# The block norms of a decoder: sums by a wide product with ones, roots on wide tiles, instead of narrow products and a chain on a few columns

## The chip, the core and the metric

The kernel runs on one core of a Trainium2 chip. The core has five engines that work through their own queues, each in order: TensorE (PE in the profile; its weight loads are shown as PEld), VectorE (DVE), ScalarE (ACT), GpSimd (POOL) and SyncE (SP), which here issues transfers. They meet through semaphores. Operands lie in SBUF, products land in the eight banks of PSUM. The metric is the device time of one launch in microseconds (us); lower is better.

## The reference, cut to what matters

Two layers over 528 tokens (16 meta tokens and 512 others) of width 1024: a gated linear attention layer, then a sliding-window attention layer. Each layer has a half-step SwiGLU block, a mixer, and another half-step SwiGLU block, and each of these six blocks has a norm ahead of it and one behind it.

```python
def rmsnorm(x, g):
    xf = x.astype(jnp.float32)
    y = xf * lax.rsqrt(jnp.mean(xf * xf, axis=-1, keepdims=True) + EPS)
    return (y * g.astype(jnp.float32)).astype(x.dtype)
...
    for layer in range(DEPTH):
        g = norm_gains[layer]
        h = h + 0.5 * rmsnorm(swiglu(rmsnorm(h, g[0]), w_ffn_in[layer, 0], w_ffn_out[layer, 0]), g[1])
        hn = rmsnorm(h, g[2])
        ...
        h = h + rmsnorm(mix, g[3])
        h = h + 0.5 * rmsnorm(swiglu(rmsnorm(h, g[4]), w_ffn_in[layer, 1], w_ffn_out[layer, 1]), g[5])
        if layer == N_A_LAYERS - 1:
            k_sh, v_sh = shared_kv(h, kv_norm, w_kv, cos, sin)
```

What matters here is `rmsnorm` over the 1024 features of each token. The linear attention has a further norm per head over 256 features (`g_head`), which the change leaves as it is.

## The kernel before

Activations are kept transposed: the residual `H` and a block's output `Y` are tiles of 128 partitions by 8 slices by 528 tokens, so that a token is a column and its 1024 features lie on 128 partitions and 8 slices. A norm therefore has to add over partitions, and its factor has to be the same on all partitions of a column.

Every block product is made of three TensorE instructions of the rounded type fp32r: weights and activations are split into a high part (a copy on ScalarE) and a low part (the difference, on VectorE), and high x high, low x high and high x low are added in PSUM (`mm3s`). The large SwiGLU products use seven half-size products instead of eight (`Strassen`); their operands are called a, c, d and e.

Tokens are worked on in two groups: 0 to 271 and 272 to 527 in the first layer (272 and 256 tokens), 16 to 271 and 272 to 527 in the second (256 each). The last products of a block run for group 0 first and for group 1 then, and the first products of the next block (`x_first`) in the same order, so that the norm of one group runs while TensorE multiplies for the other.

A pre-norm scales nothing ahead of the products: `Operand.build` writes H times gain, split in two, and the root factor of each token is put into a tile R (`Operand.factors`), with which the results are multiplied when they are taken out of PSUM (the evacuations). A post-norm (`Residual.run`) multiplies Y by its factor, adds that to H, and builds the next block's operand slice by slice, eight slices k for a group.

The sums of squares are gathered by `square_into`: ScalarE squares each slice, GpSimd adds slices 0 to 6 into one tile `acc_..._0`, and the last slice has its own tile `acc_..._7`. Two tiles with 128 partitions of partial sums are left. From there `rstd` goes in three trips:

- narrow products `st`: for every chunk of 68 or 128 tokens, each tile of sums is loaded as weights and one column of ones is moved, which gives the sums with tokens on partitions (a tile of 68 x 4 or 128 x 2);
- a root of ten small operations on that tile (a guess from the bits and two steps of refinement), on VectorE for post-norms and for the opening, on GpSimd for the other pre-norms, with ScalarE taking the sum out of PSUM; then `dg`, which spreads the factors onto a diagonal;
- the product `r`: ones as weights, `dg` moved as n fp32 columns, which puts each token's factor on all partitions. It stays in PSUM; a pre-norm copies it to R.

The order of the work is the program's own. `Flow` keeps a clock that every product pushes on; jobs (generators) `yield` a delay and come up again when the clock has passed it, between the products of the block that is being issued. `DCHAIN` and `CHAIN` are the delays between `st` and `r` (for the root on VectorE and on GpSimd), `FACT` is the one ahead of a pre-norm's sums. A job's instructions stand in each engine's queue where it came up.

Names in the profile: `acc_post`, `st_post_l0m`, `r_post_l0m` belong to a post-norm (l0m: the one whose result is the next operand l0m), `acc_l0m`, `st_l0m`, `r_l0m` to a pre-norm; `t_...` is a post-norm's scaled output, `x_l0m` an operand's slices, `x` the first products of a block, `y` its last ones, `gu` the gate and up parts. In the profile l0f stands for both SwiGLU operands of the first layer, l1f for those of the second. ScalarE needs a table load (ACT_TABLE_LOAD) when the next function isn't in the loaded table; such loads are put into the program when it is built.

Of the kernel before, what the change touches and what calls it, by code (L numbers as in the profile page):

```python
# [40 lines left out]
DCHAIN = 3.0  # L41
FACT = 1.5
# [83 lines left out]
def trunk_kernel(ctx: ExitStack, tc, a, out):  # L126
# [19 lines left out]
    def ps(name):  # L146
        return pp.tile([P, 512], F32, tag="ps", name=name)
# [203 lines left out]
    def rstd(sq, n, dim, half, name, eng=pool):  # L351
# [11 lines left out]
        if eng is dve:  # L363
            dve.tensor_scalar(aa, st[:c, :nch], 1.0 / dim, 1e-6, op0=ALU.mult, op1=ALU.add)
        else:
            act.activation(aa, st[:c, :nch], AF.Identity, scale=1.0 / dim, bias=eps[:c])
        eng.tensor_scalar(yy.bitcast(I32), aa.bitcast(I32), -0.5, RSQRT_MAGIC, op0=ALU.mult, op1=ALU.add)

        eng.tensor_tensor(zz, yy, yy, op=ALU.mult)
        eng.tensor_tensor(zz, zz, aa, op=ALU.mult)  # L370
        eng.tensor_scalar(ww, zz, 0.375, -1.25, op0=ALU.mult, op1=ALU.add)
        eng.tensor_tensor(ww, ww, zz, op=ALU.mult)
        if eng is dve:
            dve.scalar_tensor_tensor(yy, ww, 1.875, yy, op0=ALU.add, op1=ALU.mult)
            dve.tensor_tensor(zz, yy, yy, op=ALU.mult)
            dve.scalar_tensor_tensor(zz, zz, -0.5, aa, op0=ALU.mult, op1=ALU.mult)
            dve.scalar_tensor_tensor(yy, zz, 1.5, yy, op0=ALU.add, op1=ALU.mult)
        else:
            pool.tensor_scalar(ww, ww, 1.875, None, op0=ALU.add)
            pool.tensor_tensor(yy, yy, ww, op=ALU.mult)  # L380
            pool.tensor_tensor(zz, yy, yy, op=ALU.mult)
            pool.tensor_tensor(zz, zz, aa, op=ALU.mult)
            pool.tensor_scalar(zz, zz, -0.5, 1.5, op0=ALU.mult, op1=ALU.add)
            pool.tensor_tensor(yy, yy, zz, op=ALU.mult)
        dg = sm.tile([P, 272], F32, tag="dg", name=f"dg_{name}", bufs=2)
        eng.tensor_tensor(
            dg[:c, :n].rearrange("p (j c) -> p j c", c=c),
            (hident if half else ident)[:c, :c].unsqueeze(1).to_broadcast([c, nch, c]),
# [3 lines left out]
        yield DCHAIN if eng is dve else CHAIN  # L392
        r = ps(f"r_{name}")
        mm(r[:, :n], ones[:c, :], dg[:c, :n])
        return r

# [16 lines left out]
    class Operand:  # L413
# [25 lines left out]
        def factors(self, gi, eng=pool):  # L439
# [11 lines left out]
    class Residual:  # L451
        def __init__(self, name, layer, i, half, nxt=None):
            self.name, self.half, self.nxt = name, half, nxt
            self.gain = lambda m: gain(layer, i, m)
# [942 lines left out]
```

## Time and profile before

| | |
|---|---|
| median of 3 runs | 1922.35 us (1922.07 to 1923.58) |
| profiled execution | 1923.81 us |
| its span on the core | 1922.0 us |
| mean granted TensorE clock | 0.993 of full |
| TensorE busy | 1886.6 us |
| VectorE, ScalarE, GpSimd busy | 1340.6, 993.8, 342.2 us |
| table loads on ScalarE | 7, of 1283 ns each |

The span is what the profiler saw on the core; the profiled execution's own time has 1.8 us around it. Busy times are sums over instructions of one engine; products are pipelined, so that what a product costs its successors is read from the distance of starts rather than from its own length. A wait is put down to what came last.

### The profile page before, as it was taken

What the parts mean: (1) busy time and instruction counts of PE and PEld (TensorE: products, weight loads), DVE (VectorE), ACT (ScalarE), POOL (GpSimd) and SP (SyncE); (2) the same over time, 40 slices, a digit from 0 to 9 for tenths busy, and PEclk for the clock granted to TensorE, in tenths of its full rate; (3) what the DMA queues carried; (4) which work ended last, traced back from release to release, by engine and by line L of the source; (5) the groups of instructions that cost most, each with busy time, mean ns of one, the idle gap of its engine ahead of it and who ended that gap; (6) DMA issues with size and microseconds to landing.
All of it is one profiled execution on the core that took longest, in us unless ns stands there. A gap on an engine that the chain in (4) does not pass through costs nothing.

```text
span 1922.0 us, 37874 instructions
## 1 busy us (share of the span) xinstructions
PE 1886.6 (98%) x14522; PEld 1800.2 (94%) x14522; DVE 1340.6 (70%) x2724; ACT 993.8 (52%) x2268; POOL 342.2 (18%) x561
## 2 busy tenths in 40 slices
PE   8999999999999999999999999999998999999997
PEld 8999999999999999999999898989976898989897
DVE  7884848676364787575877775858678778758484
ACT  5662626553245556353674563636645665636363
POOL 2101010311111400101034011010352141010102
PEclk9999999999999999999999999999998999999998
DMA  5555556222113245555542356565321215565651
GB/s 180 149 154 141 154 143 171 96 78 77 35 56 111 64 113 149 149 149 149 159 161 56 98 146 157 143 159 165 111 67 34 71 47 128 148 150 159 152 143 45
DMA packets 133253, 231.29 MB, mean 120 GB/s; under 512 B 14928, under 2 KB 27728, under 8 KB 133072
## 3 DMA queue, kind: packets, MB, share of 16 engines
q1 hardware_dynamic: 112048, 190.99, 30.8%
q0 software_dynamic: 20736, 37.76, 12.4%
q8 instruction: 113, 1.85, 0.4%
q14 instruction: 68, 0.56, 0.1%
q10 hardware_dynamic: 288, 0.13, 0.0%
HBM read 226.72 MB, written 2.10 MB: 119 GB/s over the span
## 4 chain that ended last, share of the span: by engine, by line
PE 89%; DVE 5%; ACT 2%; POOL 1%; issue 1%; DMA 0%; SPq 0%; DVEq 0%; POOLq 0%; ACTq 0%
PE y L164 31%; PE a L164 21%; PE x L164 16%; PE c L164 9%; PE d L164 5%; PE o L164 1%; DVE w L229 1%; PE e L164 1%; PE po L164 1%; ACT w L228 1%; PE sc L164 1%; PE ps L164 0%; DVE x_l0f L429 0%; PE st_go L164 0%; DVE H L468 0%
## 5 line engine op out<-in xcount | busy, mean ns | idle before, releaser
L254 POOL DMA_DIRECT2D raw<-in_w_in x144 | 126.1, 934 | 968.8 <-DMA raw<-in_w_in 530.0
L249 DVE TENSOR_TENSOR w_s<-raw,w_s 128x512 fp32r<-128x512 f32 x288 | 195.0, 689 | 109.3 <-ACT w_s L248 107.7
L164 PE MATMUL y<-hidl0f,w 128*128 128x272 f32 (+1 forms) x2112 | 260.9, 285 | 0.0
L164 PEld LDWEIGHTS y<-hidl0f,w 128*128 128x128 f32 x2112 | 258.8, 188 | 0.2
L229 DVE TENSOR_TENSOR w<-raw,w 128x512 fp32r<-128x512 f32 x378 | 243.4, 672 | 21.0 <-ACT w L228 19.1
L164 PE MATMUL y<-hidl1f,w 128*128 128x512 f32 (+1 forms) x1344 | 249.5, 346 | 0.0
L164 PEld LDWEIGHTS y<-hidl1f,w 128*128 128x128 f32 x1344 | 212.2, 188 | 33.4 <-ACT hidl1f L410 0.3
L248 ACT ACTIVATE w_s<-raw 128x512 fp32r<-128x512 f32 x288 | 177.7, 625 | 109.0 <-DVE raw L264 69.3
L228 ACT ACTIVATE w<-raw 128x512 fp32r<-128x512 f32 x378 | 208.1, 587 | 35.0 <-PE y L164 29.3
L249 DVE TENSOR_TENSOR w<-raw,w 128x512 fp32r<-128x512 f32 x216 | 145.4, 688 | 37.6 <-ACT w L248 35.9
L164 PE MATMUL x<-x_l0m,w 128*128 128x272 f32 (+1 forms) x1200 | 158.3, 288 | 0.0
L248 ACT ACTIVATE w<-raw 128x512 fp32r<-128x512 f32 x216 | 130.4, 621 | 48.0 <-PE y L164 44.6
L164 PEld LDWEIGHTS x<-x_l0m,w 128*128 128x128 f32 x1200 | 149.4, 188 | 1.2
L590 DVE TENSOR_TENSOR Y<-y,Y 128x256 f32<-128x256 f32 (+2 forms) x176 | 82.2, 474 | 92.3 <-PE y L164 91.9
L164 PE MATMUL a<-zl0f_t,w_s 128*128 128x264 f32 x864 | 117.0, 285 | 0.0
L164 PE MATMUL a<-zl1f_t,w_s 128*128 128x256 f32 x864 | 114.3, 281 | 0.8 <-ACT c L783 0.8
L164 PEld LDWEIGHTS a<-zl0f_t,w_s 128*128 128x128 f32 x864 | 110.1, 188 | 0.0
L164 PEld LDWEIGHTS a<-zl1f_t,w_s 128*128 128x128 f32 x864 | 107.0, 188 | 2.0 <-ACT c L783 2.0
L164 PE MATMUL x<-x_l0f,w 128*128 128x256 f32 (+1 forms) x768 | 101.1, 292 | 7.4 <-ACT w L228 6.1
L406 POOL TENSOR_TENSOR acc_post<-acc_post,sq_post 128x256 f32<-128x256 f32 (+1 forms) x72 | 58.0, 805 | 280.5 <-ACT sq_post L405 280.0
L164 PEld LDWEIGHTS x<-x_l0f,w 128*128 128x128 f32 x768 | 97.8, 194 | 8.6 <-ACT w L228 6.1
L164 PE MATMUL x<-x_l1f,w 128*128 128x256 f32 (+1 forms) x576 | 92.9, 320 | 0.0
(487 smaller groups left out, 3404.4 us busy)
## 6 DMA issues: line engine op xcount, KB each, us to landing
raw<-in_w_in SPq DMA_DIRECT2D x424, 256.0 KB, 3.6
raw<-in_w_in POOLq DMA_DIRECT2D x144, 256.0 KB, 4.9
raw<-in_w_out SPq DMA_DIRECT2D x96, 256.0 KB, 3.4
raw<-in_gla_in SPq DMA_DIRECT2D x50, 256.0 KB, 3.1
raw<-in_w_last SPq DMA_DIRECT2D x48, 256.0 KB, 3.3
raw<-in_w_out SPq DMA_DIRECT2D x64, 128.0 KB, 2.9
raw<-in_gla_out SPq DMA_DIRECT2D x16, 256.0 KB, 2.7
raw<-in_w_q SPq DMA_DIRECT2D x16, 256.0 KB, 4.0
```

What stands on the lines that cost most here:

```text
L164: inst = pe.matmul(o, lhs, rhs, start=start, stop=stop, skip_group_check=onto)
L228: act.activation(w[:, 0, :m], raw[:, :m], AF.Copy)
L229: dve.tensor_tensor(w[:, 1, :m], raw[:, :m], w[:, 0, :m].bitcast(F32), op=ALU.subtract)
L248: act.activation(w[:, 0, :512], src, AF.Copy)
L249: dve.tensor_tensor(w[:, 1, :512], src, w[:, 0, :512].bitcast(F32), op=ALU.subtract)
L254: pool.dma_start(dst, src, accum_op=ALU.add)
L406: pool.tensor_tensor(sums[0][:, :n], sums[0][:, :n], t[:, :n], op=ALU.add)
L590: dve.tensor_tensor(y, p[:, :n], y, op=ALU.add)
```

## The change

The norms over 1024 features (24 counted by group: 12 behind blocks, 12 ahead of them) get a new function `roots`. The two tiles of sums are now the moved operand: ones (128 x 128) as weights, n fp32 columns of each tile, both added in one bank. That gives each token's sum on all partitions at once, so that `dg` and `r` fall away. The root is taken on the wide tile: ScalarE's function Abs_reciprocal_sqrt gives a first value, its square on ScalarE and three VectorE operations refine it by one step, and the factor one half of a half-step block is a constant of the refinement. The result lies in SBUF: for a pre-norm in R itself, for a post-norm in the tile that held the last sum. In `Residual.run` the scaled output t takes turns in the two halves of the bank that held the sums.

The delays change: the roots come up `SUMMED` = 2.5 after the sums (it was 3.0 or 5 up to r), and a pre-norm's sums come up `FACT` = 5.0 after its last slice (it was 1.5). The per-head norms of the linear attention (`rstd`, names `go`) stay on GpSimd.

```diff
--- before.py
+++ after.py
@@ -38,8 +38,8 @@
 CHAINS = 2
 
 CHAIN = 5
-DCHAIN = 3.0
-FACT = 1.5
+SUMMED = 2.5
+FACT = 5.0
 START = 1.0
 SECOND = 6.0
 STATE_KEYS = 1.5
@@ -348,7 +348,7 @@
         mm3s([(o, w)], j, x, g, start, stop)
 
 
-    def rstd(sq, n, dim, half, name, eng=pool):
+    def rstd(sq, n, dim, name):
         c = 128 if n % 128 == 0 else n // 4
         nch = n // c
         st = ps(f"st_{name}")
@@ -360,39 +360,44 @@
         zv = sm.tile([P, 4], F32, tag="zv", name=f"zv_{name}")
         wv = sm.tile([P, 4], F32, tag="wv", name=f"wv_{name}")
         aa, yy, zz, ww = av[:c, :nch], yv[:c, :nch], zv[:c, :nch], wv[:c, :nch]
-        if eng is dve:
-            dve.tensor_scalar(aa, st[:c, :nch], 1.0 / dim, 1e-6, op0=ALU.mult, op1=ALU.add)
-        else:
-            act.activation(aa, st[:c, :nch], AF.Identity, scale=1.0 / dim, bias=eps[:c])
-        eng.tensor_scalar(yy.bitcast(I32), aa.bitcast(I32), -0.5, RSQRT_MAGIC, op0=ALU.mult, op1=ALU.add)
-
-        eng.tensor_tensor(zz, yy, yy, op=ALU.mult)
-        eng.tensor_tensor(zz, zz, aa, op=ALU.mult)
-        eng.tensor_scalar(ww, zz, 0.375, -1.25, op0=ALU.mult, op1=ALU.add)
-        eng.tensor_tensor(ww, ww, zz, op=ALU.mult)
-        if eng is dve:
-            dve.scalar_tensor_tensor(yy, ww, 1.875, yy, op0=ALU.add, op1=ALU.mult)
-            dve.tensor_tensor(zz, yy, yy, op=ALU.mult)
-            dve.scalar_tensor_tensor(zz, zz, -0.5, aa, op0=ALU.mult, op1=ALU.mult)
-            dve.scalar_tensor_tensor(yy, zz, 1.5, yy, op0=ALU.add, op1=ALU.mult)
-        else:
-            pool.tensor_scalar(ww, ww, 1.875, None, op0=ALU.add)
-            pool.tensor_tensor(yy, yy, ww, op=ALU.mult)
-            pool.tensor_tensor(zz, yy, yy, op=ALU.mult)
-            pool.tensor_tensor(zz, zz, aa, op=ALU.mult)
-            pool.tensor_scalar(zz, zz, -0.5, 1.5, op0=ALU.mult, op1=ALU.add)
-            pool.tensor_tensor(yy, yy, zz, op=ALU.mult)
+        act.activation(aa, st[:c, :nch], AF.Identity, scale=1.0 / dim, bias=eps[:c])
+        pool.tensor_scalar(yy.bitcast(I32), aa.bitcast(I32), -0.5, RSQRT_MAGIC, op0=ALU.mult, op1=ALU.add)
+
+        pool.tensor_tensor(zz, yy, yy, op=ALU.mult)
+        pool.tensor_tensor(zz, zz, aa, op=ALU.mult)
+        pool.tensor_scalar(ww, zz, 0.375, -1.25, op0=ALU.mult, op1=ALU.add)
+        pool.tensor_tensor(ww, ww, zz, op=ALU.mult)
+        pool.tensor_scalar(ww, ww, 1.875, None, op0=ALU.add)
+        pool.tensor_tensor(yy, yy, ww, op=ALU.mult)
+        pool.tensor_tensor(zz, yy, yy, op=ALU.mult)
+        pool.tensor_tensor(zz, zz, aa, op=ALU.mult)
+        pool.tensor_scalar(zz, zz, -0.5, 1.5, op0=ALU.mult, op1=ALU.add)
+        pool.tensor_tensor(yy, yy, zz, op=ALU.mult)
         dg = sm.tile([P, 272], F32, tag="dg", name=f"dg_{name}", bufs=2)
-        eng.tensor_tensor(
+        pool.tensor_tensor(
             dg[:c, :n].rearrange("p (j c) -> p j c", c=c),
-            (hident if half else ident)[:c, :c].unsqueeze(1).to_broadcast([c, nch, c]),
+            hident[:c, :c].unsqueeze(1).to_broadcast([c, nch, c]),
             yy.unsqueeze(2).to_broadcast([c, nch, c]),
             op=ALU.mult,
         )
-        yield DCHAIN if eng is dve else CHAIN
+        yield CHAIN
         r = ps(f"r_{name}")
         mm(r[:, :n], ones[:c, :], dg[:c, :n])
         return r
+
+
+    def roots(sums, n, c, name, dst=None):
+        s = ps(f"st_{name}")
+        for i, t in enumerate(sums):
+            mm(s[:, :n], ones, t[:, :n], i == 0, i == len(sums) - 1)
+        yield SUMMED
+        q, y = sums[0][:, :n], sums[1][:, :n] if dst is None else dst
+        act.activation(y, s[:, :n], AF.Abs_reciprocal_sqrt, scale=1.0 / D, bias=eps)
+        act.activation(q, y, AF.Square, scale=D ** -0.5)
+        dve.scalar_tensor_tensor(q, s[:, :n], D * 1e-6, q, op0=ALU.add, op1=ALU.mult)
+        dve.tensor_scalar(q, q, -0.5 * c, 1.5 * c, op0=ALU.mult, op1=ALU.add)
+        dve.tensor_tensor(y, q, y, op=ALU.mult)
+        return y, s
 
 
     def square_into(sums, src, i, count, name):
@@ -436,13 +441,12 @@
             o, n = self.groups[gi]
             square_into(self.accs[gi], H[:, k, o : o + n], k, KD, f"{self.name}_{o}_{k}")
 
-        def factors(self, gi, eng=pool):
+        def factors(self, gi):
             if self.rt is None:
                 self.rt = sm.tile([P, TOK], F32, tag="R", name=f"R_{self.name}", bufs=2)
             o, n = self.groups[gi]
             yield FACT
-            r = yield from rstd(self.accs[gi], n, D, False, f"{self.name}_{o}", eng)
-            act.activation(self.rt[:, o : o + n], r[:, :n], AF.Copy)
+            yield from roots(self.accs[gi], n, 1.0, f"{self.name}_{o}", self.rt[:, o : o + n])
 
         def need(self, gi, k):
             flow.until(lambda: (gi, k) in self.ready)
@@ -450,21 +454,22 @@
 
     class Residual:
         def __init__(self, name, layer, i, half, nxt=None):
-            self.name, self.half, self.nxt = name, half, nxt
+            self.name, self.c, self.nxt = name, 0.5 if half else 1.0, nxt
             self.gain = lambda m: gain(layer, i, m)
 
         def run(self, gi, g, sums):
             o, n = g
             nxt = self.nxt
             yield 1.8
-            r = yield from rstd(sums, n, D, self.half, f"post_{self.name}{gi}", dve)
+            r, s = yield from roots(sums, n, self.c, f"post_{self.name}{gi}")
             if nxt is None:
                 yield from self.store(gi, g, r)
                 return
             for k in range(KD):
                 h, y = H[:, k, o : o + n], Y[:, k, o : o + n]
-                t = r[:, 256 : 256 + n] if n <= 256 else ps(f"t_{self.name}{gi}{k}")[:, :n]
-                dve.tensor_tensor(t, y, r[:, :n], op=ALU.mult)
+                c = k % 2 * 256
+                t = s[:, c : c + n] if n <= 256 else ps(f"t_{self.name}{gi}{k}")[:, :n]
+                dve.tensor_tensor(t, y, r, op=ALU.mult)
                 dve.tensor_tensor(h, t, h, op=ALU.add)
                 nxt.build(gi, k)
                 nxt.sumsq(gi, k)
@@ -473,7 +478,7 @@
 
         def store(self, gi, g, r):
             o, n = g
-            rb = r[:, :n].unsqueeze(1).to_broadcast([P, 2, n])
+            rb = r.unsqueeze(1).to_broadcast([P, 2, n])
             for k in range(0, KD, 2):
                 h, y = H[:, k : k + 2, o : o + n], Y[:, k : k + 2, o : o + n]
                 last = gi == 1 and k < 4
@@ -984,7 +989,7 @@
                         square_into(accs[gi], Y[:, 2 * h + i, o : o + n], i, 2, f"go{h}_{gi}")
                 yield 2.0
                 def scale(gi, o, n):
-                    r = yield from rstd(accs[gi], n, 256, True, f"go{h}_{gi}")
+                    r = yield from rstd(accs[gi], n, 256, f"go{h}_{gi}")
                     dve.tensor_tensor(
                         yy[:, :, o : o + n], yy[:, :, o : o + n],
                         r[:, :n].unsqueeze(1).to_broadcast([P, 2, n]), op=ALU.mult,
@@ -1242,7 +1247,7 @@
             x.sumsq(gi, k)
             yield 0.4
         yield START
-        yield from x.factors(gi, dve)
+        yield from x.factors(gi)
 
     def second():
         for k in range(KD):
```

On TensorE, among the first products of group 0 of the attention block (l1m), the rows before are these; `st_l1m` are the pre-norm's narrow products of group 0, `st_post_l1m` the post-norm's of group 1:

```order
L164 MATMUL x_2_0_17289<-x_l1m_17112,w_0_16908 128x256
L164 MATMUL st_l1m_17317<-ones,acc_l1m_0_17090 128x1
L164 MATMUL st_l1m_17317<-ones,acc_l1m_7_17259 128x1
L164 MATMUL st_l1m_17317<-ones,acc_l1m_0_17090 128x1
L164 MATMUL st_l1m_17317<-ones,acc_l1m_7_17259 128x1
L164 MATMUL st_post_l1m_17340<-ones,acc_post_0_1_17019 128x1
L164 MATMUL st_post_l1m_17340<-ones,acc_post_7_1_17271 128x1
L164 MATMUL st_post_l1m_17340<-ones,acc_post_0_1_17019 128x1
L164 MATMUL st_post_l1m_17340<-ones,acc_post_7_1_17271 128x1
L164 MATMUL x_0_0_17288<-x_l1m_17138,w_0_16793 128x256 x2
```

and in the change:

```order
L164 MATMUL x_0_0_17016<-x_l1m_16853,w_0_16535 128x256
L164 MATMUL st_post_l1m_17053<-acc_post_0_1_16761,ones 128x256
L164 MATMUL st_post_l1m_17053<-acc_post_7_1_16999,ones 128x256
L164 MATMUL st_l1m_17056<-acc_l1m_0_16811,ones 128x256
L164 MATMUL st_l1m_17056<-acc_l1m_7_16980,ones 128x256
L164 MATMUL x_0_0_17016<-x_l1m_16853,w_0_16591 128x256
L164 MATMUL x_2_0_17017<-x_l1m_16853,w_0_16623 128x256
```

Eight narrow products have become four wide ones, and the two r products, which stood 33 and 45 block products further on, are gone from the queue; the pre-norm's sums now follow the post-norm's.

On ScalarE, where the second SwiGLU block of the first layer (l0f) begins, before, from the last slice of group 1 (x_l0f_7) to the first Silu of group 1:

```order
L428 ACTIVATE x_l0f_7_8036<-H,vec 128x256
L402 ACTIVATE acc_l0f_272_7_8307<-H 128x256
L228 ACTIVATE w_0_8339<-raw_0_8205 128x512
L228 ACTIVATE w_1_8342<-raw_512_8207 128x512
L366 ACTIVATE av_l0f_272_8353<-st_l0f_272_8348,eps 128x2
L228 ACTIVATE w_0_8380<-raw_0_8209 128x512
L228 ACTIVATE w_1_8383<-raw_512_8211 128x512
L445 ACTIVATE R_l0f_8074<-r_l0f_272_8444 128x256
L644 ACTIVATE gu<-gu 128x256
L410 ACTIVATE hidl0f_0_7997<-gu 128x256
```

and in the change, where x_l0f_7 and the square of that slice (acc_l0f_272_7) stand two rows further up:

```order
L415 ACTIVATE hidl0f_1_7878<-gu 128x272
L228 ACTIVATE w_0_8155<-raw_0_8042 128x512
L228 ACTIVATE w_1_8158<-raw_512_8044 128x512
L228 ACTIVATE w_0_8173<-raw_0_8046 128x512
L228 ACTIVATE w_1_8176<-raw_512_8048 128x512
L228 ACTIVATE w_0_8191<-raw_0_8050 128x512
L228 ACTIVATE w_1_8194<-raw_512_8052 128x512
L395 ACT_TABLE_LOAD
L395 ACTIVATE R_l0f_7912<-st_l0f_272_8209,eps 128x256
L396 ACTIVATE acc_l0f_272_0_7961<-R_l0f_7912 128x256
L649 ACT_TABLE_LOAD
L649 ACTIVATE gu<-gu 128x256 x2
```

The sum's copy and the copy to R are gone; the two activations of the root stand in their place, with a table load ahead of them, and a second one follows them ahead of the next Silu. In the whole program ScalarE has 22 table loads, where it had 7: six of the added ones stand ahead of a post-norm's root of group 0, the others ahead of a pre-norm's root, a Silu or a Tanh.

At the program's end, TensorE before (`st_post_out` and `r_post_out` are the last norm's, of group 1):

```order
L164 MATMUL y_7_272_23346<-hidl1f_20_22618,w_1_22959 128x256 x3
L164 MATMUL y_7_272_23346<-hidl1f_21_22752,w_1_22959 128x256 x3
L164 MATMUL st_post_out_23369<-ones,acc_post_0_1_23156 128x1
L164 MATMUL st_post_out_23369<-ones,acc_post_7_1_23366 128x1
L164 MATMUL st_post_out_23369<-ones,acc_post_0_1_23156 128x1
L164 MATMUL st_post_out_23369<-ones,acc_post_7_1_23366 128x1
L164 MATMUL r_post_out_23390<-dg_post_out_23388,ones 128x256
```

and in the change:

```order
L164 MATMUL y_7_272_22941<-hidl1f_19_22096,w_1_22569 128x256 x3
L164 MATMUL y_7_272_22941<-hidl1f_20_22228,w_1_22569 128x256 x3
L164 MATMUL y_7_272_22941<-hidl1f_21_22362,w_1_22569 128x256 x3
L164 MATMUL st_post_out_22964<-acc_post_0_1_22766,ones 128x256
L164 MATMUL st_post_out_22964<-acc_post_7_1_22961,ones 128x256
```

VectorE at the same place in the change, from the last output slice on:

```order
L595 TENSOR_TENSOR Y<-y_7_272_22941,Y 128x256
L397 TENSOR_SCALAR acc_post_0_1_22766<-st_post_out_22964,acc_post_0_1_22766 128x256
L398 TENSOR_SCALAR acc_post_0_1_22766<-acc_post_0_1_22766 128x256
L399 TENSOR_TENSOR acc_post_7_1_22961<-acc_post_0_1_22766,acc_post_7_1_22961 128x256
L487 TENSOR_TENSOR t_out_22972<-Y,acc_post_7_1_22961 128x512
```

The program's last product is now the second product of the sums; on VectorE ten small operations and `dg` have become three wide ones.

## The prediction

> **What bounds the kernel now.** I read the page first: busy time by engine and the chain that ended last.
>
> ```profile
> PE 1886.6 (98%) x14522; PEld 1800.2 (94%) x14522; DVE 1340.6 (70%) x2724; ACT 993.8 (52%) x2268; POOL 342.2 (18%) x561
> PE 89%; DVE 5%; ACT 2%; POOL 1%; issue 1%; DMA 0%; SPq 0%; DVEq 0%; POOLq 0%; ACTq 0%
> ```
>
> TensorE is busy nearly always and carries 89% of the chain, so a product taken off its queue shortens the run unless TensorE then waits for something else. Next I read whom TensorE waits for; these are the larger waits in which a norm's own products stand at the head of its queue (us in total, times, longest).
>
> ```profile
> PE r_post_out L164 <- DVE dg_post_out L386: 2.7, 1, 2.7
> PE st_l1m L164 <- POOL acc_l1m L406: 1.1, 1, 1.1
> PE st_l0f L164 <- ACT acc_l0f L402: 1.1, 1, 1.1
> PE r_post_kv L164 <- DVE dg_post_kv L386: 0.7, 1, 0.7
> PE st_kv L164 <- POOL acc_kv L406: 0.6, 1, 0.6
> PE r_l0f L164 <- DVE dg_l0f L386: 0.6, 1, 0.6
> ```
>
> Then the timeline of TensorE through the first products of group 0 in the attention block (start, us, engine, line, operation).
>
> ```profile
> 1386.22 2.98 PE L164 MATMUL x<-x_l1m,w 128*128 128x256 f32 x24
> 1389.04 0.95 PE L164 MATMUL st_l1m<-ones,acc_l1m 128*128 128x1 f32 x8
> 1389.85 1.03 PE L164 MATMUL st_post_l1m<-ones,acc_post 128*128 128x1 f32 x8
> 1390.74 4.13 PE L164 MATMUL x<-x_l1m,w 128*128 128x256 f32 x33
> 1394.71 0.59 PE L164 MATMUL r_post_l1m<-dg_post_l1m,ones 128*128 128x256 f32 x2
> 1394.96 1.76 PE L164 MATMUL x<-x_l1m,w 128*128 128x256 f32 x12
> 1396.55 0.59 PE L164 MATMUL r_l1m<-dg_l1m,ones 128*128 128x256 f32 x2
> 1396.79 3.55 PE L164 MATMUL x<-x_l1m,w 128*128 128x256 f32 x27
> 1400.18 0.63 PE L164 MATMUL x<-zeros 128*128 128x512 f32 x2
> ```
>
> No idle time stands here: whatever the norms' products take is taken from the block's products. The first 24 give the slot of a block product, (1389.04-1386.22)/24 = 0.1175 us. All 96 of them need 11.28 us; from 1386.22 to 1400.18 are 13.96; the two norms in it cost 2.68, which is 1.34 us each.
>
> **The change part by part.** *The products.* Per norm the narrow st products (8 or 16 instructions that load a tile of sums and move one column) and the r product (2 instructions over n columns) go. In their place come two products of the kind of r: ones as weights, n fp32 columns moved, 2 instructions each. The price of r is in the same rows: from 1394.71 to 1396.55 are 1.84 us; less 12 slots (1.41) leaves 0.43. Two of them are 0.86, so a norm over 256 tokens saves 1.34 - 0.86 = 0.48 us. For 272 tokens the chain of waits has both prices:
>
> ```profile
> 360.08 0.93 PE st_post_l0m L164 x16
> ...
> 364.66 0.46 PE r_post_l0m L164 x2
> ...
> 436.59 2.12 PE ps L164 x8
> ```
>
> 0.93 + 0.46 goes, 0.92 comes: 0.47 saved. There are 24 such norms, 7 over 272 and 17 over 256 tokens; the last of the 17 stands in the tail and is counted there. 7 x 0.47 + 16 x 0.48 = 11.0 us. The pair as such is in no row. From above, the dearest fp32 product of 256 columns here is ps, 2.12/8 = 0.265 per instruction: the pair would cost 1.06 and save 0.28, over 23 norms 6.4 us. From below, four slots of a block product are 0.47: saved 0.87, over 23 norms 20 us. I take 11.0, since r is the same instruction with the same weights.
>
> *The roots.* Prices of the nearest forms (busy us, mean ns, idle before):
>
> ```profile
> L867 ACT ACTIVATE az<-z,vec 128x272 f32<-128x272 f32 x4 | 2.0, 492 | 4.1 <-PE z L164 4.1
> L405 ACT ACTIVATE sq_post<-Y 128x272 f32<-128x272 f32 x18 | 7.6, 428 | 6.2 <-DVE Y L590 5.2 <-POOL acc_post L406 0.4
> L964 DVE SCALAR_TENSOR_TENSOR st<-st,dec,ps 128x256 f32<-128x256 f32 x12 | 5.7, 476 | 0.1
> L868 DVE TENSOR_SCALAR ls<-z,vec 128x272 f32<-128x272 f32 x4 | 2.0, 496 | 1.7 <-ACT az L867 1.7
> L467 DVE TENSOR_TENSOR t_l0m<-Y,r_post_l0m 128x272 f32<-128x272 f32 x8 | 3.4, 438 | 1.5 <-PE r_post_l0m L164 1.5
> L644 ACT ACT_TABLE_LOAD x3 | 3.8, 1283 | 0.1
> ```
>
> A root is two activations (0.49 + 0.43) and three VectorE operations (0.48 + 0.50 + 0.44): 2.34 us behind the sums, with no third trip to TensorE. Twelve of them replace post-norm chains on VectorE, two the opening's, ten GpSimd's. VectorE gains and loses about the same; GpSimd is only relieved, and no DMA issue of SP or POOL is moved past anything new. The factor of a pre-norm is read by evacuations alone, and no wait of TensorE names one; it stays covered.
>
> *The table loads.* The order of ScalarE holds 22 loads instead of 7, since the new root function and Silu, Tanh or Exp take turns: 15 x 1.283 = 19.2 us more. They wait for nothing, so each runs once the activation ahead of it is done:
>
> ```profile
> 26.05 0.40 ACT L445 ACTIVATE R_l0f<-r_l0f 128x272 f32<-128x272 f32 x1 [2.88 <-PE r_l0f L164]
> 26.46 1.28 ACT L644 ACT_TABLE_LOAD   x1
> 27.76 0.76 ACT L644 ACTIVATE gu<-gu 128x272 f32<-128x272 f32 x2
> ```
>
> ScalarE idles 48% of the span. The six loads ahead of post-norms all belong to group 0, behind whose sums TensorE's queue still holds 75 to 123 block products, 9 to 14 us. The others belong to pre-norm factors and to what evacuations need, and TensorE reads neither soon. I cost them at 0; if that cover is gone, 19.2 is the other end. The Trainium skill, page "ScalarE: Activation LUTs", section "What ACT_TABLE_LOAD costs", puts a switch at 1283 ns plus a drain of 1380 ns, 2.66 us. This trace agrees with the load and shows no drain: from 26.45 to 27.76 is 1.31 us. By the page's figure the 15 would take an estimated 39.9 us of ScalarE.
>
> *The waits.* Two r waits go with their products: 0.7 + 0.6 = 1.3. The three st waits (2.8) I credit with nothing. There the last slice of group 1 is late, and TensorE needs that slice a few products further on:
>
> ```profile
> 650.00:664.00 14.00, 12.91 (x100) 12.67 (x99) 13.57 (x29) 10.91 (x25) 5.52 (x8) 0.91 0.25 78
> 1400.00:1412.00 12.00, 10.89 (x90) 10.59 (x90) 11.39 (x30) 5.14 (x12) 10.53 (x13) 1.00 0.15 44
> 660.94 0.48 DVE L429 SCALAR_TENSOR_TENSOR x_l0f<-H,vec,x_l0f 128x256 fp32r<-128x256 f32 x1
> ```
>
> The first two rows are stages (length, then busy us of PE, PEld, DVE, ACT, POOL): VectorE is busy 13.57 of 14 and 11.39 of 12 while it builds group 1. A post-norm root may start the building 2.0 us earlier (sums done at 1390.74 plus 2.34 is 1393.1, r now ends at 1394.71 + 0.43 = 1395.1), but the pre-norm root of group 0 puts 1.42 us on VectorE just there. Ends: 2.8 gained, or as much again lost.
>
> *The tail.* Behind the last block product nothing covers the chain:
>
> ```profile
> 1908.60 0.83 PE L164 MATMUL st_post_out<-ones,acc_post 128*128 128x1 f32 x6 [0.80 <-ACT acc_post L402]
> 1909.46 0.16 DVE L364 TENSOR_SCALAR av_post_out<-st_post_out 128x2 f32<-128x2 f32 x1 [1.37 <-PE st_post_out L164]
> 1912.08 1.19 PE L164 MATMUL r_post_out<-dg_post_out,ones 128*128 128x256 f32 x2 [2.65 <-DVE dg_post_out L386]
> 1913.38 2.49 DVE L482 TENSOR_TENSOR t_out<-Y,r_post_out 128x512 f32<-128x512 f32 x4 [1.45 <-PE r_post_out L164]
> ```
>
> From 1908.60 to 1913.38 is 4.78 us. Afterwards one wide product waits for the last square (its fellow is done by then): 0.86 to its reader if it lands as the narrow ones do (1908.60 to 1909.46), 1.30 if as r does (1912.08 to 1913.38), then 2.34 of root. Gain 1.1 to 1.6; I take 1.5, as TensorE has just been busy. No table load stands here: the order has the root function loaded for group 0 already.
>
> *Sum.* -11.0 - 1.3 - 1.5 = -13.8 us on the profiled execution's 1923.81 (span 1922.0 and 1.8 around it): 1910.0. The median of the runs lies 1.5 below that execution: 1922.35 - 13.8 = 1908.5, say 1908.
>
> **The rivals.**
> - *Group 1 gives it back.* If the building of group 1 on VectorE sets the end of each of the five stages that open a block, the three norms that lie in a stage save nothing: 15 x 0.48 = 7.2 lost, 1915. For it: the two stage rows. Against: in the middle of such a stage (1386 to 1400) TensorE has no gap, and the build may start earlier.
> - *The softmax stage shifts.* Its waits are set by where products stand in the queue, and the order there changes. TensorE idles 3.2 + 3.0 us in two stretches of it:
>
> ```profile
> 1430.00:1450.00 20.00, 16.80 (x76) 9.73 (x73) 19.17 (x53) 13.08 (x57) 6.56 (x6) 1.00 0.24 82
> 1470.00:1490.00 20.00, 16.99 (x146) 12.98 (x143) 17.57 (x46) 10.68 (x44) 3.71 (x3) 0.91 0.16 54
> ```
>
>   Doubled, that costs 6.2: 1915.
> - *Slower: the loads stand in line.* If every added load delays an activation on which TensorE waits, +19.2: 1908.5 + 19.2 = 1927.7. It turns the gain over from 11 bare loads of 15 (13.8/1.283). For it: ScalarE writes the high half of each slice of group 1, and is busy 10.91 of 14 there. Against: in ScalarE's order no added load stands ahead of a slice of group 1 (the Silu loads that do are there before too), so it would have to be the evacuations that hold TensorE up. By the page's 2.66 us a load the same rival would end at an estimated 1948.
>
> **How the numbers follow.** A time within 0.2% (3.8 us) of before can hardly be told from no change. Forecast 0.61; group 1 gives it back 0.18; the softmax stage 0.09; loads in line 0.12. The forecast's own range, by the ends of its terms, is 1903 (0.6 saved per norm, 1.6 in the tail, all the waits shown gone) to 1914 (the dear product, 1.1 in the tail). To leave out 2 in 10 the range must take in both middle rivals and only touch the last: 1901 to 1918. Faster is the forecast and nearly all of the two middle rivals, 0.83; within 0.2% a piece of each rival, 0.06; slower the rest, 0.11.
>
> **What would show it.** Right: TensorE's busy time falls by about 11 us; the pairs cost 0.86 to 0.92 in the chain; 22 loads of 1.28 us in ScalarE's rows; no wait on r left, save the head norms'; the last product to the first t_out in 3.2 to 3.7 us. Wrong: waits of TensorE for x in the stages that open a block, behind VectorE or ScalarE; longer waits on sc; pairs at over 1 us; activations of x late behind a load.

## The result, and the profile after

The changed kernel takes 1914.41 us (median of 6 runs, 1913.6 to 1918.1) against 1922.39 us for the kernel before on the same chip. The ratio is 0.9963, with a 95% interval of 0.995 to 0.9975. By the medians it is 8.0 us faster, by the ratio 7.1, where 13.8 were forecast. The profiled execution took 1916.86 us with a span of 1914.9; before it was 1923.81 and 1922.0, so the two profiles differ by 7.1 us of span.

The page of the kernel after, busy time by engine and the chain that ended last:

```profile
PE 1876.2 (98%) x14322; PEld 1785.4 (93%) x14322; DVE 1355.1 (71%) x2642; ACT 1026.2 (54%) x2309; POOL 316.5 (17%) x441
PE 83%; DVE 10%; ACT 4%; issue 1%; POOL 0%; DMA 0%; SPq 0%; DVEq 0%; ACTq 0%; POOLq 0%
```

TensorE's busy time fell by 10.4 us (1886.6 to 1876.2), which is the forecast for the products. But its idle time, the span less the busy time, rose from 35.4 to 38.7, and VectorE doubled its share of the chain (5% to 10%). The products came off, but more of the path that ended last now runs through VectorE. The larger waits of TensorE that are new or longer (us in total, times, longest):

```profile
PE ptm L176 <- DVE mt L1175: 5.3, 4, 2.1
PE y L164 <- ACT hidl1f L415: 2.9, 1, 2.9
PE x L164 <- ACT x_l1m L433: 1.7, 1, 1.7
PE st_post_kv L164 <- POOL acc_post L411: 1.0, 1, 1.0
```

The waits on the r of these norms and the three on pre-norm sums are gone. In their place stand a wait at the first output products of the last block (hid, the hidden values of its SwiGLU), one for a slice of the attention block's operand (x_l1m), and longer ones in the softmax stage (ptm, 0.7 before; those on sc, its score products, in the same stage fell from 6.9 to 3.8).

The timeline of TensorE that answers to the stage shown in the prediction:

```profile
1376.52 4.05 PE L164 MATMUL x<-x_l1m,w 128*128 128x256 f32 x33
1380.40 1.03 PE L164 MATMUL st_post_l1m<-acc_post,ones 128*128 128x256 f32 x4
1381.27 1.03 PE L164 MATMUL st_l1m<-acc_l1m,ones 128*128 128x256 f32 x4
1381.94 7.76 PE L164 MATMUL x<-x_l1m,w 128*128 128x256 f32 x63
1389.54 0.63 PE L164 MATMUL x<-zeros 128*128 128x512 f32 x2
```

The same 96 block products and two norms take 13.02 us (1376.52 to 1389.54), 13.96 before: 0.94 saved, 0.47 per norm. A pair costs (13.02 - 11.28)/2 = 0.87.

So the loss is elsewhere. The longest of the new waits stands at the start of the last block. First ScalarE, then TensorE, then the whole core in windows (busy us of PE, PEld, DVE, ACT, POOL, then the granted clock):

```profile
1571.60 3.22 ACT L228 ACTIVATE w<-raw 128x512 fp32r<-128x512 f32 x6
1574.84 1.28 ACT L395 ACT_TABLE_LOAD   x1
1576.13 0.47 ACT L395 ACTIVATE R_l1f<-st_l1f,eps 128x256 f32<-128x256 f32 x1
...
1592.48 3.58 PE L164 MATMUL y<-hidl1f,w 128*128 128x512 f32 x14
1598.91 5.33 PE L164 MATMUL y<-hidl1f,w 128*128 128x512 f32 x15 [2.85 <-ACT hidl1f L415]
```

```profile
1595.00:1600.00 5.00, 2.15 (x10) 1.33 (x9) 4.84 (x9) 1.94 (x5) 0.00 (x0) 1.00 0.10 39
1600.00:1605.00 5.00, 5.00 (x16) 3.93 (x15) 4.96 (x9) 4.50 (x9) 0.02 (x1) 0.66 0.68 211
```

The factor of group 1 comes late, TensorE waits 2.85 us for a slice of hid, and right behind the wait its clock falls to 0.66 over 5 us, another 1.7 us. At the first y product of this block the changed kernel was 10.95 us ahead of the one before (1603.43 and 1592.48); behind the 96 y products that come first it is 5.96 ahead (1625.63 and 1619.67).

The tail, with the line that answers to each of the prediction's:

```profile
1902.34 0.70 PE L164 MATMUL st_post_out<-acc_post,ones 128*128 128x256 f32 x2 [0.50 <-ACT acc_post L407]
1903.08 0.47 ACT L395 ACTIVATE acc_post<-st_post_out,eps 128x256 f32<-128x256 f32 x1 [0.25 <-PE st_post_out L164]
1904.09 0.42 DVE L397 SCALAR_TENSOR_TENSOR acc_post<-st_post_out,acc_post 128x256 f32<-128x256 f32 x1 [2.25 <-ACT acc_post L396]
1905.34 4.64 DVE L487 TENSOR_TENSOR t_out<-Y,acc_post 128x512 f32<-128x512 f32 x4
1906.11 3.31 POOL L488 TENSOR_TENSOR H<-t_out,H 128x512 f32<-128x512 f32 x2 [5.02 <-DVE t_out L487]
```

From the last sum to the first t_out are 3.00 us, 4.78 before: 1.78 gained. But the four t_out products take 4.64 us instead of 2.49. This was the first clue.

### The profile page after: what moved, and what is told of

The parts are those of the page before. It is cut to its first block, busy times and chain, and to the rows that moved or that the text cites. A ratio compares the mean times of both kernels' runs of the same rounds, so it can differ in the third digit from the quotient of the medians.

```text
span 1914.9 us, 37300 instructions
## 1 busy us (share of the span) xinstructions
PE 1876.2 (98%) x14322; PEld 1785.4 (93%) x14322; DVE 1355.1 (71%) x2642; ACT 1026.2 (54%) x2309; POOL 316.5 (17%) x441
## 4 chain that ended last, share of the span: by engine, by line
PE 83%; DVE 10%; ACT 4%; issue 1%; POOL 0%; DMA 0%; SPq 0%; DVEq 0%; ACTq 0%; POOLq 0%
PE y L164 29%; PE a L164 21%; PE x L164 13%; PE c L164 9%; PE d L164 5%; DVE w L229 1%; PE o L164 1%; PE e L164 1%; ACT w L228 1%; DVE H L473 1%; PE po L164 1%; PE sc L164 0%; PE ps L164 0%; DVE st_post_l1f L472 0%; PE st_go L164 0%
## 5 line engine op out<-in xcount | busy, mean ns | idle before, releaser
L164 PE MATMUL y<-hidl0f,w 128*128 128x256 f32 (+1 forms) x2112 | 260.8, 285 | 0.6 <-ACT hidl0f L415 0.6
L249 DVE TENSOR_TENSOR w<-raw,w 128x512 fp32r<-128x512 f32 x216 | 145.3, 688 | 36.9 <-ACT w L248 35.4
```

Of the source, the lines that this page charges most:

```text
L164: inst = pe.matmul(o, lhs, rhs, start=start, stop=stop, skip_group_check=onto)
L249: dve.tensor_tensor(w[:, 1, :512], src, w[:, 0, :512].bitcast(F32), op=ALU.subtract)
```

## The experiments

Three theories stood against each other. **A**: the loss sits at the start of the last block, because the root of group 1 stands late in ScalarE's queue (six weight splits and a table load are ahead of it). **B**: the table loads delay work all along the run. **C**: the factor of a post-norm now lies in SBUF (acc_post) where r lay in PSUM; a VectorE product whose two inputs are both in SBUF is slow while GpSimd works, so the building of each next operand is late. Theory C came from the sizes of the group "t<-Y,factor" in the trace of after (min/median/max in ns):

```profile
L472 DVE TENSOR_TENSOR st_post_l1m<-Y,acc_post x16: 420/478/969, 1366.0 to 1399.1; 128x256 f32<-128x256 f32 x16
L472 DVE TENSOR_TENSOR t_l0f<-Y,acc_post x8: 433/543/1024, 622.5 to 634.9; 128x272 f32<-128x272 f32 x8
L472 DVE TENSOR_TENSOR t_kv<-Y,acc_post x8: 436/836/1020, 987.7 to 999.8; 128x272 f32<-128x272 f32 x8
```

In the kernel before, no product of these groups went over 447 ns:

```profile
L467 DVE TENSOR_TENSOR t_kv<-Y,r_post_kv x8: 429/436/447, 994.2 to 1004.4; 128x272 f32<-128x272 f32 x8
```

Of the 80 products of after, 31 took over 0.5 us, and each of the 31 overlaps an instruction of GpSimd in the trace. The timeline of after shows one product without GpSimd's company and two beside it:

```profile
989.67 0.44 DVE L472 TENSOR_TENSOR t_kv<-Y,acc_post 128x272 f32<-128x272 f32 x1
...
991.15 1.74 POOL L411 TENSOR_TENSOR acc_kv<-acc_kv,sq_kv 128x272 f32<-128x272 f32 x2 [2.40 <-ACT sq_kv L410]
...
992.18 1.91 DVE L472 TENSOR_TENSOR t_kv<-Y,acc_post 128x272 f32<-128x272 f32 x2
992.45 0.51 ACT L603 ACTIVATE Y<-Y,vec 128x256 f32<-128x256 f32 x1
992.85 0.93 POOL L411 TENSOR_TENSOR acc_post<-acc_post,sq_post 128x256 f32<-128x256 f32 x1
```

All times below are given as the ratio to the kernel before on the same chip, with its 95% interval; the changed kernel itself stands at 0.9963.

**No table loads (no_loads).**

```diff
-        act.activation(y, s[:, :n], AF.Abs_reciprocal_sqrt, scale=1.0 / D, bias=eps)
+        act.activation(y, s[:, :n], AF.Identity, scale=1.0 / D, bias=eps)
...
-        dve.tensor_scalar(q, q, -0.5 * c, 1.5 * c, op0=ALU.mult, op1=ALU.add)
-        dve.tensor_tensor(y, q, y, op=ALU.mult)
+        dve.tensor_scalar(q, q, 0.0, 0.25 * c, op0=ALU.mult, op1=ALU.add)
+        dve.tensor_tensor(y, q, y, op=ALU.min)
```

> The root function is replaced by Identity, which every table set has, and the Newton step by a bounded dummy with the same instructions; the root itself is left out, so the values differ. ScalarE then holds 7 table loads instead of 22. Theory A (the loss sits where the last block opens: the root of group 1 comes late on ScalarE, TensorE waits 2.9 us for hid and then runs at half clock for another 1.7): two of the loads stand right there, 1.3 to 2.6 us earlier, so the wait shrinks to 0.3 to 1.6 us and the clock drop goes; 1914.4 - 1.3 to 1914.4 - 4.6, so 1910 to 1913. Theory B (the loads delay work all along the run): more than that comes back, below 1908. Theory C (VectorE's products beside GpSimd are the cause): no change within 1 us, 1913.5 to 1915.

Measured: 0.9964 [0.9951, 0.9976], the same as with the loads. ScalarE is busy 18 us less (1008.2 against 1026.2), and the wait for hid at the last block is still there:

```profile
PE y L164 <- ACT hidl1f L415: 3.4, 1, 3.4
```

Theory B falls. The 15 loads cost nothing that these intervals can tell (2.5 us either way), as the prediction had it. Theory A is weakened too: two loads fewer in front of this root did not shorten the wait, though here no fall of the clock followed it.

**The sums of the pre-norms earlier (fact15).**

```diff
-FACT = 5.0
+FACT = 1.5
```

> Only FACT goes back from 5.0 to 1.5, so the sums of the pre-norms are issued 3.5 us earlier in the planner's time. Theory A: the root of group 1 is ready about 3 us earlier where the last block opens, and the wait of 2.9 us and the clock drop of 1.7 there go (-4.6), but the sums' waits for late slices come back at up to 2.8 us: 1910 to 1913. Theory B (loads): the same number of loads, 1914 to 1916. Theory C: no change there, and the sums' waits on top: 1915 to 1917.

Measured: 1.0016 [1.0008, 1.0025], slower than the kernel before, where all three theories had expected it to stay faster. Waits for slices of the sums come back, larger than they were; the wait of pk, a transpose in the linear attention, grew as well (1.3 before):

```profile
PE st_l1m L164 <- POOL acc_l1m L411: 3.7, 2, 1.9
PE pk L176 <- DVE f L920: 3.3, 1, 3.3
PE st_kv L164 <- DVE Y L595: 3.0, 1, 3.0
PE st_l0m L164 <- DVE Y L595: 2.0, 1, 2.0
```

With the post-norm factor in SBUF the slices are late, and sums issued early stand at the head of TensorE's queue waiting for them. FACT = 5.0 hides that; it is worth about 10 us here (1.0016 against 0.9963).

**The factor back in PSUM (psum_root).**

```diff
-        q, y = sums[0][:, :n], sums[1][:, :n] if dst is None else dst
+        q, y = sums[0][:, :n], dst
+        if dst is None:
+            y = s[:, 256 : 256 + n] if n <= 256 else ps(f"r_{name}")[:, :n]
...
-                c = k % 2 * 256
-                t = s[:, c : c + n] if n <= 256 else ps(f"t_{self.name}{gi}{k}")[:, :n]
+                t = s[:, :n] if n <= 256 else ps(f"t_{self.name}{gi}{k}")[:, :n]
```

> The factor of a post-norm is written to PSUM instead of SBUF (the upper half of the sums' tile, or a tile of its own for 272 tokens), as r was in the kernel before; nothing else changes. Theory C (a VectorE product whose operands are all in SBUF takes twice as long while GpSimd works: t_out 1.76 against 0.69 us in the tail, the products of group 0 and 1 up to 1.02 against 0.43): all these products are back at 0.42 to 0.45 and 0.69 us, the tail after the last product is 0.9 us shorter, and group 1 is built earlier; 1911.5 to 1913.5. Theories A and B: only the tail moves, at most 1 us, and the wait where the last block opens stays: 1913.4 to 1914.4.

Measured: 0.9911 [0.9898, 0.9925], 1905.01 us: 10 us better than the change as made, more than theory C had asked for. The edit also keeps t in the lower half of the bank, where it took turns; before_sbuf, further down, leaves t where it was. The products' sizes, the waits that are left and the tail:

```profile
L473 DVE TENSOR_TENSOR st_post_l1m<-Y,st_post_l1m x16: 409/420/430, 1361.4 to 1393.3; 128x256 f32<-128x256 f32 x16
L473 DVE TENSOR_TENSOR t_kv<-Y,r_post_kv x8: 429/433/446, 985.2 to 994.6; 128x272 f32<-128x272 f32 x8
```

```profile
PE ptm L176 <- DVE mt L1176: 5.5, 4, 2.1
PE sc L164 <- ACT s L1157: 1.6, 2, 1.4
PE r_go L164 <- POOL dg_go L377: 1.5, 1, 1.5
```

```profile
1893.33 2.49 DVE L488 TENSOR_TENSOR t_out<-Y,st_post_out 128x512 f32<-128x512 f32 x4
1894.10 2.49 POOL L489 TENSOR_TENSOR H<-t_out,H 128x512 f32<-128x512 f32 x2 [4.98 <-DVE t_out L488]
```

No product is over 446 ns, though 42 of the 80 overlap an instruction of GpSimd by more than 0.1 us. The waits for hid, x_l1m and st_post_kv are gone with ScalarE's queue and its loads unchanged, so theory A named the place and not the cause: the root at the last block was late because the slices that it sums were late. The time from ScalarE's write of the last slice to the root is the same in both kernels, 8.85 us in the changed one (1567.28 to 1576.13) and 8.86 here (1557.52 to 1566.38). But TensorE reaches its first y product 25.20 us behind that slice there (1592.48) and 27.75 here (1585.27). In the tail VectorE and GpSimd are both back at 2.49 us.

**GpSimd's additions left out, the factor in SBUF (no_adds).**

```diff
         act.activation(t[:, :n], src, AF.Square)
-        pool.tensor_tensor(sums[0][:, :n], sums[0][:, :n], t[:, :n], op=ALU.add)
```

> The changed kernel without GpSimd's six additions per norm (the sums hold the first and the last square alone, so the values differ); the factor stays in SBUF, and every other instruction stays. If the slow products come from GpSimd working beside a VectorE product whose operands are all in SBUF (theory C), the products of the groups are back at 0.42 to 0.45 us as with the factor in PSUM and the wait of 2.9 us for hid goes: the gain over before is 15 to 19 us, with the tail's last two products still slow, since GpSimd adds there. If it is the place of the operand as such, whatever GpSimd does, the products stay at up to 1 us and the gain stays at 7 to 9 us.

Measured: 0.9904 [0.9891, 0.9918], as fast as with the factor in PSUM. Without the additions the sums are ready sooner too, so the time alone would not settle it; the sizes of the products do. The operand may stay in SBUF as long as GpSimd does not work beside it:

```profile
L471 DVE TENSOR_TENSOR t_kv<-Y,acc_post x8: 440/444/449, 983.7 to 992.7; 128x272 f32<-128x272 f32 x8
```

Four of its 80 products are still over 0.6 us, beside GpSimd work that stays. It takes both, the place of the operand and GpSimd's company. That is theory C.

**The suspected cause alone, in the kernel before (before_sbuf).**

```diff
             r = yield from rstd(sums, n, D, self.half, f"post_{self.name}{gi}", dve)
...
+            rs = sums[1][:, :n]
+            act.activation(rs, r[:, :n], AF.Copy)
...
-                dve.tensor_tensor(t, y, r[:, :n], op=ALU.mult)
+                dve.tensor_tensor(t, y, rs, op=ALU.mult)
```

> The kernel before with one thing added: the post-norm's r is copied by ScalarE from PSUM into the second tile of squares, and the products of the groups read it there (the last block's stores still read PSUM). Theory C: the suspected cause alone, without any other part of the change. The copy itself puts 0.42 us ahead of ten groups' building; the slowed products make the slices late for the early narrow sums (FACT is 1.5 here): slower by 10 to 20 us, as from the post-norms changed with the factor in PSUM to the same with it in SBUF, ratio 1.005 to 1.010. If the place of the factor matters only together with the new root, within 2 us of before, 0.999 to 1.001.

Measured: 1.0104 [1.0088, 1.0119], some 20 us slower. Ten copies of 0.38 to 0.40 us, even if none were covered, would be 4.0; VectorE's waits ahead of the groups' products grew by 4.8 (14.0 to 18.8). In the profiles the span grew by 20.7 us, of which 12 are a lower clock, counted as in the last section. The products:

```profile
L469 DVE TENSOR_TENSOR t_kv<-Y,acc_post x8: 440/540/1031, 999.7 to 1011.2; 128x272 f32<-128x272 f32 x8
```

**The halves of the change (post_only, post_psum, pre_only).** In post_only Residual.run and store are those of the change, factors and rstd those of before; post_psum is the same with the psum_root edit; in pre_only the reverse holds, with FACT = 5.0. The core of post_only, in Residual.run:

```diff
-            r = yield from rstd(sums, n, D, self.half, f"post_{self.name}{gi}", dve)
+            r, s = yield from roots(sums, n, self.c, f"post_{self.name}{gi}")
```

And of pre_only, in Operand.factors:

```diff
-            r = yield from rstd(self.accs[gi], n, D, False, f"{self.name}_{o}", eng)
-            act.activation(self.rt[:, o : o + n], r[:, :n], AF.Copy)
+            yield from roots(self.accs[gi], n, 1.0, f"{self.name}_{o}", self.rt[:, o : o + n])
```

> The kernel before with the post-norms changed alone; the pre-norms keep the narrow sums, GpSimd's chain and the r product. 15 loads instead of 22. By the prediction's terms: 11 norms by 0.475 is 5.2, the tail 1.5, the r_post_kv wait 0.7: 1922.4 - 7.4 = 1915.0. Theory A (the loss comes with the pre-norm root's place on ScalarE): no loss where the last block opens, so 1915 holds or the clock gives more, 1914 to 1916. Theory B (loads): 8 loads at up to 1.28 more, above 1918. Theory C: the slow products beside GpSimd stay, 1916 to 1918.

> The post-norms changed alone, with the factor in PSUM. By theory C the 14.7 us that this half of the change cost with the factor in SBUF are all from the slowed products, which made the narrow sums of the pre-norms wait: with fast products the prediction's terms hold, 5.2 of products, 1.8 of tail, 0.7 of waits, a gain of 7 to 9 us, ratio 0.995 to 0.9965. If the narrow pre-norm sums collide with the new post-norms for another reason, it stays slower than before, ratio above 1.002.

> The pre-norms changed alone (sums by ones, root on wide tiles, FACT 5); the post-norms as before, r in PSUM. Their factor lies in SBUF in both kernels and is read by evacuations, so theory C sees no slow products. Terms: 12 norms by 0.475 is 5.7, the r waits of the opening 0.6, the three waits of the pre-norm sums 2.8: a gain of 6 to 9 us, ratio 0.995 to 0.997. If the table loads or the root's place on ScalarE cost (theories A and B, 14 more loads), less than 3 us of gain, ratio above 0.9985.

Measured: post_only 1.0082 [1.0068, 1.0095], post_psum 0.9987 [0.9978, 0.9996], pre_only 0.9987 [0.9978, 0.9996]. The first two differ only in the factor's place: 18 us, as theory C has it. But the halves alone, without slow products, bring some 2.5 us each, 5 together, where the whole with the factor in PSUM brings 17. All the expectations of 6 to 9 us were missed. Part of it can be read. From the first x product of the second block (375.95 before) to that of the third (634.87), the stage of the gated linear attention, both halves lose 2.2 us against before while psum_root gains 2.3; in pre_only the head norms and a transpose wait longer there (1.5 and 1.3 before):

```profile
PE r_go L165 <- POOL dg_go L387: 3.4, 3, 1.8
PE pk L177 <- DVE f L929: 2.7, 1, 2.7
```

In post_psum 1.7 us of that loss are a lower clock (0.96 and 0.70 in the windows from 375 to 385 us). Over the whole run up to the last product the clock takes 10.2 us from post_psum, 8.5 from before and 3.4 from pre_only, counted as in the last section. So it explains 1.7 us of what post_psum misses, and nothing of what pre_only misses, which gained 5 us by the clock. Why each half alone falls so badly into the head stages stays open.

**Early sums with fast products (psum_fact).** The psum_root edit and FACT = 1.5.

> The factor in PSUM and FACT at 1.5, as before the change. If the 11 us that FACT 1.5 cost with the factor in SBUF came because the slowed products made the slices of the groups late for early sums, then with fast products only the old waits of the sums return, about 2.8 us over the factor in PSUM with FACT 5: ratio to before 0.9925 (a gain of 14 us). If early sums cost by themselves, 11 us come off the gain of 18: ratio 0.996 to 0.997.

Measured: 0.9918 [0.9904, 0.9931], within 2 us of FACT = 5.0. So the 10 us of fact15 came with the slowed products.

**Each pair issued twice (twice_psum).** The psum_root edit, and:

```diff
-        for i, t in enumerate(sums):
-            mm(s[:, :n], ones, t[:, :n], i == 0, i == len(sums) - 1)
+        for i, t in enumerate(sums + sums):
+            mm(s[:, :n], ones, t[:, :n], i % 2 == 0, i % 2 == 1)
```

> The factor in PSUM, and each norm's pair of products issued twice (the second pair starts the sum anew, so the values stay). If the pair costs what the prediction took, 0.86 us over 256 tokens and 0.92 over 272, and nothing hides it, the doubling takes 24 x 0.88 = 21 us away from the gain of 18: slower than before by about 3 us, ratio 1.001 to 1.003. If the pairs run beside waits that are there anyway, less than 14 us goes, ratio below 0.9985. If the pair were as dear as 1.06, 25 us go, ratio above 1.0035.

Measured: 0.996 [0.9947, 0.9974], so 9.4 us went (against 0.9911), not 21:

```profile
PE 1890.3 (99%) x14418; PEld 1802.8 (94%) x14418; DVE 1334.5 (70%) x2642; ACT 1026.2 (54%) x2309; POOL 311.1 (16%) x441
PE ptm L176 <- DVE mt L1176: 2.5, 1, 2.5
...
1369.98 1.89 PE L164 MATMUL st_post_l1m<-acc_post,ones 128*128 128x256 f32 x8
1371.52 14.94 PE L164 MATMUL y<-hidl1f,w 128*128 128x256 f32 x123
```

TensorE's busy time rose by 19.3 us (1871.0 to 1890.3). Of these 3.4 are a lower clock (6.8 us against 3.4 up to the last product), which leaves 0.66 for each of the 24 added pairs. The last two rows agree: two pairs take 1.54 us from start to start, where one takes 0.87 in the stage of the result, so the second costs 0.67. A pair behind its like is thus cheaper here than one that stands alone, and the doubling does not test the forecast's 0.86. TensorE's idle time fell by 4.6 us (30.9 to 26.3), as the ptm wait halved: time put on TensorE ahead of that stage was in part taken out of its waits.

**Both values of FACT (l1m_early).** The psum_root edit, and:

```diff
-            yield FACT
+            yield 1.5 if self.name == "l1m" else FACT
```

> The factor in PSUM with FACT 5, but 1.5 for the operand of the attention block alone. With FACT 1.5 everywhere the stage from the first product of that block to the first of the next was 2.8 us shorter than with 5, while the GLA stage was 4.2 longer. If each stage's waits depend on its own order of products, the two best are had together: the gain of 18 us grows by up to 2.8, ratio 0.9895 to 0.991. If the stage's gain came from what lies ahead of it, no change: 0.991 to 0.9915.

Measured: 0.9886 [0.9873, 0.99], 1901.06 us. This is the fastest version measured, 22 us under the kernel before and about 15 us (0.9886 against 0.9963) under the change. Its margin over psum_root, 0.0025, is about as large as the intervals, and the two ran on different chips, so it is likely and not shown. In the profiles the stage from the attention block's first x product to that of the last block is 1.2 us shorter than in psum_root (164.20 against 165.37), with 3.4 us more lost to the clock in it.

## Why the prediction was right and wrong

The forecast was -13.8 us; -8.0 were measured by the medians and -7.1 by the ratio and by the two profiles. The sign and the range held; the gain was little more than half. In the profiles TensorE's busy time fell by 10.4 us, where the sum had 11.0, but its idle time rose by 3.3, where the sum took 2.8 off (1.3 of waits and 1.5 of tail).

- *The products, -11.0.* Right: TensorE's busy time fell by 10.4, at the same loss of clock in both profiles, and the stage shown gives 0.47 per norm where 0.47 to 0.48 was forecast.
- *The roots, "VectorE gains and loses about the same; GpSimd is only relieved".* This is the step that failed. It priced the instructions that the change adds and not those that read their result. The row quoted for the products, L467 at 438 ns, had r in PSUM; the change puts the factor into SBUF, so both inputs lie there, and 80 products and 8 t_out, whose sum was some 40 us, took 54.5 us, up to 1.02 and 1.76 us a piece. With that alone undone the gain is 17 us, and TensorE's idle time falls by 4.5 us; with that alone done to the kernel before, some 20 us are lost. The Trainium skill, page "SBUF — State Buffer", section "Who interferes with whom", states just this rule: a VectorE instruction with two SBUF inputs contends with a GpSimd instruction that reads SBUF, and one with at most one SBUF input, outside the modes in which it takes both ports, does not. The runs agree (at most 447 ns with one input in PSUM, up to 1024 with both in SBUF). It speaks against this change, and the prediction does not weigh it.
- *"The factor of a pre-norm is read by evacuations alone … it stays covered".* Wrong at one place, the last block, where 2.85 us of wait went and 1.7 of clock behind it. But with the factor in PSUM the sentence holds: psum_root has no such wait.
- *The table loads, 0.* Right, by no_loads. By the 1.28 us of a row they add 19.2 us to ScalarE; it is busy 18 us more with them, and no time comes of it that the intervals can tell.
- *The waits, -1.3 for r and nothing for st.* The r waits went. For the st waits the ends given were 2.8 gained or lost. With slow products the answer hangs on FACT (fact15), which the prediction did not weigh at all; with fast ones they all went at FACT = 5.0, the good end.
- *The tail, -1.5.* The chain to the first t_out gave 1.78, then the t_out products gave 0.9 back. From the start of the last block product to the end of the span it was 14.64 us and is 13.76.
- *The rivals.* "Group 1 gives it back" named the outcome (1915) and the engine, VectorE building the next operand, but not the mechanism: the building did start earlier, as the argument against it said, but 31 of the 80 products in it were slowed. "The softmax stage shifts": ptm rose from 0.7 to 5.3, but from the first x product of the attention block to the first of the last block are 168.07 us (1376.52 to 1544.59) against 167.57, so it took 0.5. "Loads in line" fell.

Had the factor stayed in PSUM, the forecast of 13.8 would have been too small: 17 were measured. In the profiles psum_root has 20.1 us less span than before: 4.5 of idle time, 15.6 of busy time. Of the latter about 10.5 are the products, and 5.1 are clock. No term of the forecast holds the clock, so that part is luck as far as the forecast goes; without it 15.0 of the 20.1 remain, near the 13.8.

## What to carry to other kernels

When a change moves a value to another memory, price again every instruction that reads it, not only those that write it, and look at what GpSimd does in the same stretch. Here a maximum of twice the minimum within one group was the sign of the collision: read the spread of a group, not only its mean. And a constant that sets how far ahead work is issued, as FACT does, may hide a slow producer; vary it alone before trusting either.

## What the runs showed of the hardware

*VectorE and GpSimd.* With both inputs in SBUF a VectorE product of 256 or 272 columns takes 0.42 to 0.45 us alone and up to 1.03 beside GpSimd's addition; of 512 columns, 0.69 alone and 1.76. With one input in PSUM it stays at 0.41 to 0.45 and 0.69, also where GpSimd works. One input in SBUF is not safe for every operation: the root's own TENSOR_SCALAR (L398 in after), from SBUF to SBUF, takes 0.29 us, and 6 of its 24 took 0.50 to 0.82, all of them beside GpSimd. GpSimd suffers too: the two H additions of the tail took 3.31 us beside the slow products, 2.49 else.

*The clock after short gaps.* A gap of TensorE can be dearer than its length. In the kernel before, one wait of 1.09 us is followed by a window at a lower clock:

```profile
660.94 0.89 PE L164 MATMUL st_l0f<-ones,acc_l0f 128*128 128x1 f32 x6 [1.09 <-ACT acc_l0f L402]
...
660.00:665.00 5.00, 4.06 (x21) 4.06 (x22) 3.95 (x7) 3.16 (x8) 2.29 (x7) 0.66 0.63 193
```

Over 5 us a clock of 0.66 loses 5 x 0.34 = 1.7 us. Summed so over windows of 5 us up to the last product, before and after lose 8.5 us each, in four places, psum_root 3.4, in one. In these three profiles each loss is 1.7 or 3.4, behind gaps between 1.1 and 2.9 us. But a gap's length does not decide it. The gap at r_go, 1.5 to 1.6 us in all three, has a loss of 1.7 behind it in after and none in the other two, and in no_loads the wait for hid has none either:

```profile
1596.75 7.47 PE L164 MATMUL y<-hidl1f,w 128*128 128x512 f32 x31 [3.44 <-ACT hidl1f L415]
...
1600.00:1605.00 5.00, 5.00 (x24) 4.04 (x23) 4.97 (x9) 4.95 (x11) 1.72 (x2) 1.00 0.85 270
```

The Trainium skill, page "TensorE: Matmul & The Clock Gate", section "HAM oscillation — how this bites in real kernels", warns of gaps over some 3.4 us; here the clock fell behind gaps of a third of that and did not fall behind this one of 3.44, and the measurement decides. What does decide stays open, and no run set a gap on its own. A wait taken away can be worth more than its length, and one that is added can cost more, but a profile shows one execution, and the next may lose more or less.
